# Reading the moving operand of the large matmuls in turns of four columns from its two halves

## The chip, the cores and the metric

The kernel runs on one core of one Trainium2 chip. The metric is device time in microseconds (us) for one launch. The time before is the median of two runs, 2388.72 us (2388.01 and 2389.42).

## The reference

The reference is one step of a two-layer transformer trunk in float32, applied to two groups of 128 tokens: a prompt, which has no cached context, and a sample, which has 128 cached positions. Layer 0 mixes tokens by latent attention and grouped-query attention side by side, layer 1 by differential attention; each layer ends with a gated feed-forward block with a width-3 convolution over positions. Cut to the parts that carry the work:

```python
for l in range(DEPTH):                                   # 2 layers
    mod = jax.nn.silu(cond) @ w_ada[l] + b_ada[l]        # 2048 x 12288, one row per group
    sh1, sc1, gt1, sh2, sc2, gt2 = jnp.split(mod[:, None, :], 6, axis=-1)
    h = rmsnorm(x, g_norm_mix[l]) * (1 + sc1) + sh1
    m, new = mixer_ab(h, ...) if l % 2 == 0 else mixer_c(h, ...)   # w_in, attention, w_out
    x = x + gt1 * m
    h = rmsnorm(x, g_norm_ffn[l]) * (1 + sc2) + sh2
    u = h @ w_ffn_up[l]                                  # 2048 x 11264
    u = conv3(u) + b
    x = x + gt2 * ((silu(gate) * val) @ w_ffn_down[l])   # 5632 x 2048
return rmsnorm(x, g_final), ab_ctx, c_ctx
```

Both groups use the same weights, so the kernel lays the two groups' 128 tokens beside each other: 256 columns, the first 128 for the prompt and the last 128 for the sample.

## The kernel before

**The product.** All large weight matrices are multiplied by `gemm` (lines 300 to 314) or, for the first three output blocks of a stage, by `first_three` (lines 279 to 298). An output block is 128 features by 256 tokens and is summed in one PSUM tile `acc` over blocks of 128 input features. To get near float32 accuracy out of the fp32r format, weights and activations are each split into a high and a low part. Each input block then takes three matmuls: high weights by high activations (L309, in `first_three` L295), high weights by low activations (L310, L296) and low weights by high activations (L313, L297). In each, the weights (128x128, `wh` or `wl`) are the stationary operand, loaded by a weight load of their own, and the activations (128x256) are the moving operand that streams past them. The moving operand is the tile `hx` (normalised input, also the attention output of layer 0), `g` (the gated hidden features), `oall` (attention output of layer 1) or `ql` (query latents), each with 256 high columns followed by 256 low ones for a block. One tile, `kv_in`, has 384 columns, since cached positions stand between the two groups.

**Where the operands lie.** Within a partition the high half of a moving operand is 256 contiguous float32 values, 1024 bytes, of which each group's 128 columns are 512 bytes. One weight block is 128 contiguous values, 512 bytes. The pools hold small tiles named `pad` (among them `SHIFT // 4` columns in L659, L910 and L1023, beside 48 columns in L112), and in the built program every moving operand of these matmuls begins at a byte address of 96 modulo 512 and every weight block at 160 modulo 512. `hx`, for one, lies at 42592, and the four buffers of `wh` at 118944, 123040, 127136 and 131232.

**What feeds it.** SyncE issues one DMA of 1 MB for each sixteen weight blocks (`raw`). ScalarE rounds 1024 columns of it to fp32r (`wh`, L216) and VectorE subtracts to get the low part (`wl`, L217). Four buffers each of `wh` and `wl` and three of `raw` lie between these engines and TensorE. Results leave PSUM through ScalarE or VectorE: a convolution with three taps in the feed-forward block (L1030, L1033, L1036), an addition into `x` behind the second product (L586).

**What stands between.** The modulation vectors `mod` need `w_ada`, 2048 x 12288 for each layer. Its work is strewn between the large products by `pump`, `row_step` and `feature_step`: some on TensorE (L434, plain float32 products with 32 weight columns), some on VectorE (L419, L463). Attention's own products (L635, L951, L970 and their neighbours) are plain float32.

**What sets the order.** The order on each engine comes from a planner that works from program order and a model of costs; some instructions are pinned to program order. The planner's order for the changed kernel is the same, instruction for instruction, on TensorE, VectorE, ScalarE, GpSimd and SyncE; besides the access patterns only a few waits on an engine that another wait already covers differ.

Of the kernel before, what the change touches and what calls it, by code (L numbers as in the profile page):

```python
# [20 lines left out]
T = 128  # L21
NT = 2 * T
ROW = 2 * NT
SHIFT = 448
NL = 2
GRID_W = 64
EPS = 1e-6
# [11 lines left out]
    ("rch", 128), ("rsh", 128), ("rcm", 128), ("rsm", 128),  # L39
    ("cond", 32), ("bada", NL * 6 * KD),  # L40
    ("gmix", NL * KD), ("gffn", NL * KD), ("gfin", 16),
    ("gmq", 6), ("gmkv", 4), ("gqn", 1), ("gkn", 1), ("lam", 4),
# [41 lines left out]
def step_kernel(ctx: ExitStack, tc: tile.TileContext, A: dict):  # L84
    nc = tc.nc
    pe, dve, act, pool, sp = nc.tensor, nc.vector, nc.scalar, nc.gpsimd, nc.sync
# [16 lines left out]
    def nm(s):  # L103
        uid[0] += 1
        return f"{s}_{uid[0]}"

    def T_(pl, shape, tag, dt=F32, bufs=None):
        kw = {} if bufs is None else {"bufs": bufs}
        return pl.tile(shape, dt, tag=tag, name=nm(tag), **kw)
# [8 lines left out]
    def C(name):  # L118
        a, w = _AT[name]
        return cst[:, a:a + w]  # L120
# [8 lines left out]

    mod = T_(keep, [P, NL, 6, KD, 2], "mod")  # L130
    scl = T_(keep, [P, NL, 2, KD, 2], "scl")

# [53 lines left out]
    def bank():  # L186
        return T_(pmisc, [P, 512], "misc")

    def att_bank():
        return T_(ppool["att"], [P, 512], "att", bufs=3)  # L190
# [30 lines left out]
    class Weights:  # L221
# [29 lines left out]
        def chunk(self):  # L251
# [24 lines left out]
            out, self.blocks = self.blocks[:self.nblk], self.blocks[self.nblk:]  # L276
            return out

    def first_three(W, xh, xl, order, mid=None, fixed=False):


        pin = tc.keep_in_program_order if fixed else lambda i: i
        raws = [W.load() for _ in range(3)]
        ps = [T_(pacc, [P, 512], "acc") for _ in range(3)]
        blocks = {(c, h): W.halves(raws[c], 8 * h) for c, h in ((0, 0), (1, 0), (2, 0), (0, 1))}
        count = [0] * 3
        for n, (c, k) in enumerate(order):
            if mid and n == len(order) // 2:
                mid()
            if (c, k // 8) not in blocks:  # L290
                blocks[c, k // 8] = W.halves(raws[c], 8)
            wh, wl = blocks[c, k // 8][k % 8]
            a, b = count[c] == 0, count[c] == KD - 1
            count[c] += 1
            pin(pe.matmul(ps[c][:, :NT], wh, xh(k), start=a, stop=False))  # L295
            pin(pe.matmul(ps[c][:, :NT], wh, xl(k), start=False, stop=False))  # L296
            pin(pe.matmul(ps[c][:, :NT], wl, xh(k), start=False, stop=b))  # L297
        return [p[:, :NT] for p in ps]

    def gemm(blocks, xh, xl, n=NT, first=0, between=None):  # L300


        fixed = lambda i: tc.keep_in_program_order(i) if between else i
        ps = T_(pacc, [P, 512], "acc")
        last = len(blocks) - 1
        for i in range(last + 1):
            k = (i + first) % (last + 1)
            wh, wl = blocks[k]
            fixed(pe.matmul(ps[:, :n], wh, xh(k), start=(i == 0), stop=False))  # L309
            fixed(pe.matmul(ps[:, :n], wh, xl(k), start=False, stop=False))  # L310
            if between and i == (last + 1) // 2:
                between()
            fixed(pe.matmul(ps[:, :n], wl, xh(k), start=False, stop=(i == last)))  # L313
        return ps[:, :n]


# [37 lines left out]
    def vector(name, l, j, q):  # L354

        at = (l * _AT[name][1] // NL) + j * KD + 4 * q
        return C(name)[:, at:at + 4, None].to_broadcast([P, 4, 2])
# [186 lines left out]
    def modulated(st, l, which, W, fixed):  # L544
# [29 lines left out]
        def turn():  # L574
            rest[1](tc.keep_in_program_order)

        ps = first_three(W, lambda k: hx[:, k, :NT], lambda k: hx[:, k, NT:2 * NT],
                         AS_MADE if fixed else IN_TURN, lambda: sum_rows(2, raws[2]), fixed)
        if fixed:
# [75 lines left out]
    def mixer_ab(hx, rb0, st):  # L655
        l = 0
        with tc.tile_pool(name="ab", bufs=1) as ab:
            with tc.tile_pool(name="abp", bufs=1) as pj:
                T_(ab, [P, SHIFT // 4], "pad")  # L659
                kv_in = T_(ab, [P, 4, 2, 3 * T], "kv_in", F32R)  # L660
# [104 lines left out]
                def part(W, k0, n, first, rate, between=None, **kw):  # L765

                    for c in range(23):
                        ps = gemm(W.chunk(), lambda k: hx[:, k0 + k, :NT], lambda k: hx[:, k0 + k, NT:2 * NT])
                        to = pr[:, c] if c < 15 else qb[:, c - 15]
                        if first:  # L770
                            act.copy(to, ps)
                        else:
                            dve.tensor_tensor(out=to, in0=to, in1=ps, op=ALU.add)
                        if between:
                            between(c)
                        pump(rate, **kw)
# [34 lines left out]
            with tc.tile_pool(name="abh", bufs=1) as hp:  # L811
# [35 lines left out]
                for h in range(8):  # L847
                    if h % 2 == 0:
                        for i in range(2):
                            ps = gemm(WQ.chunk(), qh, qlo)  # L850
                            qn[h + i] = T_(hp, [P, NT], "qn", bufs=4)
                            act.copy(qn[h + i], ps)
                            pump(RATE["heads"])
                        ps = gemm(WQ.chunk(), qh, qlo)
                        ev = T_(tmp, [P, NT], "nt", bufs=4)
                        act.copy(ev, ps)
                        qr = T_(hp, [P, NT], "qr", bufs=2)
                        act.copy(qr[:, 0:T], ev[:, 0:T])
                        rope(qr[:, None, T:], ev[:, None, T:], 1, 32, "rcm", "rsm")
                        pump(RATE["heads"])  # L860
# [34 lines left out]
    def mixer_c(cp, hx, W, ready, todo, st):  # L895
# [13 lines left out]
        product = lambda: ready.pop(0) if ready else gemm(W.chunk(), xh, xl, between=todo.pop(0) if todo else None)  # L909
        T_(cp, [P, SHIFT // 4 - 24], "pad")  # L910
        o_all = T_(cp, [P, KD, ROW], "oall", F32R)
# [90 lines left out]
        W = Weights(A["w_out_c"], KD, 1)  # L1002
        oh, ol = (lambda k: o_all[:, k, :NT]), (lambda k: o_all[:, k, NT:2 * NT])
        ready = first_three(W, oh, ol, LAST_LATE)
        for c in range(KD):
            fine[0] = c >= KD - QUIET[2]
# [8 lines left out]
    def ffn(hx, W, ready, todo, l, st):  # L1015
# [4 lines left out]
        with tc.tile_pool(name=f"ffn{l}", bufs=1) as fp, banks(f"pffn{l}") as pf:  # L1020
            feat["home"], feat["pool"] = fp, pf
            feat["due"] = 0.0
            T_(fp, [P, SHIFT // 4], "pad")  # L1023

# [53 lines left out]
    with banks("pab") as ppool["ada"]:  # L1078
# [4 lines left out]
        ps = [bank(), att_bank()]  # L1083
# [75 lines left out]
def _layout(i):  # L1159
# [29 lines left out]

    a["w_ada"] = i["w_ada"].reshape(NL, 4, 4, P, 6, 4, 512).transpose(0, 4, 5, 1, 3, 2, 6).copy()  # L1190
    for j in (1, 0):
# [60 lines left out]
```

## Time and profile before

| what | value |
|---|---|
| runs | 2388.01 and 2389.42 us, median 2388.72 |
| span of the profiled execution, first to last instruction | 2384.0 us |
| median of the runs less that span | 4.7 us |
| TensorE matmuls busy (union of overlapping matmuls) | 2333.9 us, 98% |
| TensorE weight loads busy | 2201.5 us, 92% |
| VectorE busy | 1775.5 us, 74% |
| ScalarE busy | 1164.9 us, 49% |
| DMA | 612.94 MB, mean 257 GB/s |
| mean granted TensorE clock | 0.994 |

The profile gives no time of the profiled execution other than its span; the 4.7 us around it are taken from the runs. Matmuls are pipelined: one is listed with some 0.28 us while the next begins 0.11 us after it. The busy share of TensorE therefore says whether the engine was ever without a matmul, and not how fast matmuls follow each other; that is read from the starts of neighbouring rows in the timeline.

### The profile page before, as it was taken

How to read it: one execution, taken by the hardware profiler on the slowest of the kernel's cores; microseconds unless marked ns; L12 is line 12 of the kernel's file. 1: busy time of each engine (PE TensorE's matmuls, PEld its weight loads, DVE VectorE, ACT ScalarE, POOL GpSimd, SP SyncE). 2: the span in 40 equal slices, each digit the busy share in tenths (PEclk: the TensorE clock that was granted, in tenths of full speed). 3: DMA queues.
4: the chain of work that ended last, by engine and by line, in shares of the span. 5: the costliest groups of instructions: out<-in, count | busy, mean ns of one | idle time of the engine just before them, and what ended most of it. 6: DMA issues, size and time to landing. Idle time of an engine off the chain costs nothing. (4 is left out here: it accounts for less than half of the span.)

```text
span 2384.0 us, 47535 instructions
## 1 busy us (share of the span) xinstructions
PE 2333.9 (98%) x19784; PEld 2201.5 (92%) x19784; DVE 1775.5 (74%) x2720; ACT 1164.9 (49%) x1817; POOL 167.6 (7%) x205
## 2 busy tenths in 40 slices
PE   8999999999999999999999999999999999999997
PEld 6778868789999999999989999998999999999997
DVE  2667545569999999999979777878899855666654
ACT  4345544365554345554455444445655534555542
POOL 0001101100000000001220000023000000000011
PEclk9999999999999999999999999999999999999999
DMA  8886678877777876777766787776767655555553
GB/s 347 352 336 250 226 282 310 317 269 260 261 253 282 296 278 252 265 263 270 297 238 235 277 295 293 257 300 265 257 250 261 212 194 193 193 194 193 194 194 123
DMA packets 92551, 612.94 MB, mean 257 GB/s; under 512 B 9969, under 2 KB 17841, under 8 KB 20529
## 3 DMA queue, kind: packets, MB, share of 16 engines
q1 hardware_dynamic: 92336, 609.91, 69.7%
q8 instruction: 155, 2.54, 0.4%
q14 instruction: 60, 0.48, 0.1%
HBM read 605.12 MB, written 4.75 MB: 256 GB/s over the span
## 5 line engine op out<-in xcount | busy, mean ns | idle before, releaser
L216 ACT CAST wh<-raw 128x1024 fp32r<-128x1024 f32 (+1 forms) x788 | 793.7, 1013 | 963.8 <-PE acc L310 803.0
L217 DVE TENSOR_TENSOR wl<-raw,wh 128x1024 fp32r<-128x1024 f32 (+1 forms) x788 | 921.2, 1182 | 368.9 <-ACT wh L216 363.1
L309 PE MATMUL acc<-hx,wh 128*128 128x256 f32 x4064 | 1132.3, 279 | 10.9 <-ACT wh L216 4.2
L313 PE MATMUL acc<-hx,wl 128*128 128x256 f32 x4064 | 1129.1, 278 | 0.8 <-DVE wl L217 0.8
L310 PE MATMUL acc<-hx,wh 128*128 128x256 f32 x4064 | 1128.3, 278 | 0.0
L309 PEld LDWEIGHTS acc<-hx,wh 128*128 128x128 f32 x4064 | 764.4, 188 | 40.9 <-issue 16.3
L313 PEld LDWEIGHTS acc<-hx,wl 128*128 128x128 f32 x4064 | 764.3, 188 | 11.8 <-issue 8.7
L310 PEld LDWEIGHTS acc<-hx,wh 128*128 128x128 f32 x4064 | 764.9, 188 | 9.4 <-issue 7.9
L310 PE MATMUL acc<-g,wh 128*128 128x256 f32 x1408 | 388.3, 276 | 0.0
L313 PE MATMUL acc<-g,wl 128*128 128x256 f32 x1408 | 388.0, 276 | 0.0
L309 PE MATMUL acc<-g,wh 128*128 128x256 f32 x1408 | 387.8, 276 | 0.0
L419 DVE CUSTOM_DVE_ANT_0 junk<-araw,condb 128x2048 f32<-128x2048 f32 x120 | 274.6, 2289 | 0.0
L310 PEld LDWEIGHTS acc<-g,wh 128*128 128x128 f32 x1408 | 264.3, 188 | 0.0
L313 PEld LDWEIGHTS acc<-g,wl 128*128 128x128 f32 x1408 | 264.1, 188 | 0.0
L309 PEld LDWEIGHTS acc<-g,wh 128*128 128x128 f32 x1408 | 264.0, 188 | 0.0
L172 POOL TENSOR_TENSOR sqacc<-sqacc,sq 128x256 f32<-128x256 f32 x62 | 82.0, 1322 | 1521.7 <-issue 1216.1
L463 DVE SCALAR_TENSOR_TENSOR aacc<-araw,condw,aacc 128x512 f32<-128x512 f32 x150 | 111.3, 767 | 0.2
L586 DVE SCALAR_TENSOR_TENSOR x<-acc,mod,x 128x128 f32<-128x128 f32 x192 | 58.1, 343 | 56.0 <-PE acc L313 55.0
L1030 ACT ACTIVATE cv<-acc,convw 128x256 f32<-128x256 f32 x176 | 98.3, 558 | 1.4 <-PE acc L297 1.4
L434 PE MATMUL ada<-araw,condw 128*32 128x512 f32 x704 | 94.6, 614 | 3.8 <-DMA araw<-w_ada 3.0
L1036 DVE SCALAR_TENSOR_TENSOR cv<-acc,convw,cv 128x254 f32<-128x254 f32 x176 | 84.2, 479 | 3.5
L1033 DVE SCALAR_TENSOR_TENSOR cv<-acc,convw,cv 128x254 f32<-128x254 f32 x176 | 83.5, 475 | 2.6 <-ACT cv L1030 2.5
(236 smaller groups left out, 1893.0 us busy)
## 6 DMA issues: line engine op xcount, KB each, us to landing
araw<-w_ada SPq DMA_DIRECT2D x186, 1024.0 KB, 5.8
raw<-w_up SPq DMA_DIRECT2D x176, 1024.0 KB, 4.8
raw<-w_down SPq DMA_DIRECT2D x88, 1024.0 KB, 4.8
raw<-w_in_c SPq DMA_DIRECT2D x48, 1024.0 KB, 5.3
raw<-w_in_ab SPq DMA_DIRECT2D x19, 1024.0 KB, 7.0
raw<-w_out_ab SPq DMA_DIRECT2D x16, 1024.0 KB, 6.8
raw<-w_out_c SPq DMA_DIRECT2D x16, 1024.0 KB, 4.8
raw<-w_ada SPq DMA_DIRECT2D x6, 1024.0 KB, 9.9
```

Source lines behind the costliest of these rows:

```text
L172: pool.tensor_tensor(out=st["acc"], in0=st["acc"], in1=sq, op=ALU.add)
L216: pin(act.copy(out_hi, src))
L217: pin(dve.tensor_tensor(out=out_lo, in0=src, in1=out_hi.bitcast(F32), op=ALU.subtract))
L309: fixed(pe.matmul(ps[:, :n], wh, xh(k), start=(i == 0), stop=False))
L310: fixed(pe.matmul(ps[:, :n], wh, xl(k), start=False, stop=False))
L313: fixed(pe.matmul(ps[:, :n], wl, xh(k), start=False, stop=(i == last)))
L419: tc.keep_in_program_order(dve.tensor_tensor_reduce(out=T_(feat["pool"], [P, D], "junk"), in1=feat["row"][:, c], in0=feat["raw"].rearrange ...
L434: i = pe.matmul(ada["ps"][32 * g:32 * g + 32, :], condw[:, 4 * t + g, :], raw[:, g], start=(t == 0), stop=(t == 3), skip_group_check=True)
L463: i = dve.scalar_tensor_tensor(out=acc[:, c], in0=raw[:, g], scalar=condw[:, k, c:c + 1], in1=acc[:, c], op0=ALU.mult, op1=ALU.add)
L1030: pin(act.activation(y, ps, AF.Identity, scale=cw[:, 1, m:m + 1], bias=cw[:, 3, m:m + 1]))
L1033: pin(dve.scalar_tensor_tensor(out=y3[:, :, 1:], in0=p3[:, :, :T - 1], scalar=cw[:, 0, m:m + 1], in1=y3[:, :, 1:], op0=ALU.mult, op1=ALU.add))
L1036: pin(dve.scalar_tensor_tensor(out=y3[:, :, :T - 1], in0=p3[:, :, 1:], scalar=cw[:, 2, m:m + 1], in1=y3[:, :, :T - 1], op0=ALU.mult, op1=A ...
```

## The change

The 256 columns of a moving operand are no longer read from first to last. They are read in turns of four: columns 0 to 3 of the first half, columns 0 to 3 of the second half, columns 4 to 7 of the first half, and so on, 64 turns in all. The output pattern is permuted in the same way, so each result lands in the same place of PSUM as before. For `kv_in` the turns go over three blocks of 128. The weight operand, the number of instructions and all other instructions stay as they are. Half the lines added are the same edit in `first_three`.

```diff
+RUN = 4
...
+    def paired(ap):
+
+        return ap.rearrange("p (j i e) -> p i j e", i=T // RUN, e=RUN)
+
...
+            out = paired(ps[c][:, :NT])
-            pin(pe.matmul(ps[c][:, :NT], wh, xh(k), start=a, stop=False))
+            pin(pe.matmul(out, wh, paired(xh(k)), start=a, stop=False))
...
         ps = T_(pacc, [P, 512], "acc")
+        out = paired(ps[:, :n])
         last = len(blocks) - 1
         for i in range(last + 1):
             k = (i + first) % (last + 1)
             wh, wl = blocks[k]
-            fixed(pe.matmul(ps[:, :n], wh, xh(k), start=(i == 0), stop=False))
-            fixed(pe.matmul(ps[:, :n], wh, xl(k), start=False, stop=False))
+            fixed(pe.matmul(out, wh, paired(xh(k)), start=(i == 0), stop=False))
+            fixed(pe.matmul(out, wh, paired(xl(k)), start=False, stop=False))
             if between and i == (last + 1) // 2:
                 between()
-            fixed(pe.matmul(ps[:, :n], wl, xh(k), start=False, stop=(i == last)))
+            fixed(pe.matmul(out, wl, paired(xh(k)), start=False, stop=(i == last)))
         return ps[:, :n]
```

More of the change, by code (lines that the diff above doesn't have):

```diff
@@ L294, in first_three @@
             count[c] += 1
-            pin(pe.matmul(ps[c][:, :NT], wh, xh(k), start=a, stop=False))
-            pin(pe.matmul(ps[c][:, :NT], wh, xl(k), start=False, stop=False))
-            pin(pe.matmul(ps[c][:, :NT], wl, xh(k), start=False, stop=b))
+            out = paired(ps[c][:, :NT])
+            pin(pe.matmul(out, wh, paired(xh(k)), start=a, stop=False))
+            pin(pe.matmul(out, wh, paired(xl(k)), start=False, stop=False))
+            pin(pe.matmul(out, wl, paired(xh(k)), start=False, stop=b))
         return [p[:, :NT] for p in ps]
```

## The prediction

> **What bounds the kernel now.** First the page's busy times, then two long stretches of the windows view, taken from the feed-forward blocks, then TensorE's waits.
>
> ```profile
> span 2384.0 us, 47535 instructions
> PE 2333.9 (98%) x19784; PEld 2201.5 (92%) x19784; DVE 1775.5 (74%) x2720; ACT 1164.9 (49%) x1817; POOL 167.6 (7%) x205
> PEclk9999999999999999999999999999999999999999
> ```
>
> ```profile
> core 0: us, PE busy (x) PEld busy (x) DVE busy (x) ACT busy (x) POOL busy (x), PEclk, DMA share, GB/s
> 700.00:1100.00 400.00, 400.00 (x3532) 400.00 (x3531) 368.05 (x462) 195.26 (x250) 0.00 (x0) 1.00 0.74 272
> 1700.00:2300.00 600.00, 600.00 (x5297) 600.00 (x5296) 428.28 (x558) 298.65 (x388) 6.73 (x5) 1.00 0.60 212
> ```
>
> ```profile
> PE misc L1088 <- ACT sq L1086: 6.7, 1, 6.7
> PE acc L309 <- ACT wh L216: 4.2, 2, 2.7
> PE att L197 <- ACT sq L168: 3.9, 3, 2.4
> ```
>
> TensorE is without a matmul for only 2384.0 - 2333.9 = 50 us, and its longest waits in all are a few us each, so nothing upstream sets the time. In both stretches matmuls follow each other at the same pace, 400/3532 = 0.113 us and 600/5297 = 0.113 us, although VectorE is busy 92% in one and 71% in the other, and DMA 0.74 and 0.60. The clock is at its full grant. The pace of a large product is thus a property of the product, and the end is set by that pace times their number. The timeline gives the pace more exactly (the 54 starts from the first row to the last all belong to such products):
>
> ```profile
> 999.80 0.28 PE L310 MATMUL acc<-hx,wh 128*128 128x256 f32 x1
> ...
> 1000.03 0.28 PE L309 MATMUL acc<-hx,wh 128*128 128x256 f32 x1
> ...
> 1005.92 0.28 PE L310 MATMUL acc<-hx,wh 128*128 128x256 f32 x1
> ```
>
> (1005.92 - 999.80)/54 = 0.1133 us for 256 columns, 0.443 ns a column. [...]
>
> How many there are, from the groups by line and shape. L310 and L313 have the count of L309, and L295 and L297 that of L296:
>
> ```profile
> L309 PE MATMUL acc<-hx,wh 128*128 128x256 f32 x4064 | 1132.3, 279 | 10.9 <-ACT wh L216 4.2 <-ACT hx L537 2.5 <-ACT cv L1030 2.5
> L309 PE MATMUL acc<-g,wh 128*128 128x256 f32 x1408 | 387.8, 276 | 0.0
> L309 PE MATMUL acc<-oall,wh 128*128 128x256 f32 x208 | 57.9, 279 | 0.0
> L296 PE MATMUL acc<-hx,wh 128*128 128x256 f32 x144 | 41.4, 293 | 3.1 <-POOL hx L522 2.7
> L309 PE MATMUL acc<-ql,wh 128*128 128x256 f32 x72 | 20.8, 288 | 0.0
> L296 PE MATMUL acc<-oall,wh 128*128 128x256 f32 x48 | 14.0, 293 | 0.0
> L309 PE MATMUL acc<-kv_in,wh 128*128 128x384 f32 x64 | 22.7, 355 | 0.0
> ```
>
> Three times (4064 + 1408 + 208 + 144 + 72 + 48) = 17,832 products of 256 columns, 2021 us at 0.1133, or 85% of the span; and 192 of 384 columns. One nanosecond more or less a product is 17.8 us.
>
> **Is there anything to gain in 0.1133?** Two comparisons say that there is. The 384-column products, ten steps apart, and attention's plain float32 products among the large ones:
>
> ```profile
> 229.21 0.34 PE L310 MATMUL acc<-kv_in,wh 128*128 128x384 f32 x1
> ...
> 230.94 0.34 PE L313 MATMUL acc<-kv_in,wl 128*128 128x384 f32 x1
> ```
>
> ```profile
> 1251.61 1.47 PE L951 MATMUL att<-dk,dq 128*128 128x128 f32 x8
> ```
>
> ```profile
> L951 PE MATMUL att<-dk,dq x64: 270/327/382, 1251.6 to 1536.7; 128*128 128x128 f32 x32, 128*128 128x256 f32 x32
> ```
>
> 384 columns take 0.173 us: half as many columns again cost 0.060 us more, 0.467 ns each, above the mean of 0.443 of the first 256. So a constant cost per product is not all that stands over the columns; something grows with them. The eight float32 passes (four of 128 columns, four of 256) start over 1.47 - 0.38 = 1.09 us before the last one; that is ten times 128 columns, 0.109 us each. A float32 pass streams at half the fp32r pace, so 128 of its columns take as many steps as 256 here, and it has a 128-column weight load beside it too. It needs 4.3 ns less.
>
> What differs? A weight load's duration grows from 32 to 128 columns as follows:
>
> ```profile
> L434 PEld LDWEIGHTS ada<-araw,condw 128*32 128x32 f32 x704 | 14.5, 108 | 19.3 <-issue 6.1 <-DMA araw<-w_ada 3.2 <-DVE scl L400 1.2
> L309 PEld LDWEIGHTS acc<-g,wh 128*128 128x128 f32 x1408 | 264.0, 188 | 0.0
> ```
>
> (188 - 108)/96 = 0.83 ns a column, 107 ns for a block. During one product, therefore, weights are read through 512 bytes once, while the moving operand passes through 1024 bytes. Both begin at fixed places modulo 512 (96 and 160). I read the excess as the two readers of SBUF meeting: modulo 512 the moving reader goes at twice the weight reader's speed and overtakes it once a product, and a 384-column one overtakes more often. In the float32 pass both go through 512 bytes in the same time and neither overtakes. This reading is inferred; no row shows a bank.
>
> **The change part by part.** *Reading.* The halves lie 512 bytes apart, so a turn of four from each keeps both on one place modulo 512, which moves through 512 bytes once a product: the speed of the weight reader. They start 64 bytes apart and stay so; if they do touch, a stall draws them apart, and they don't catch up again. On this reading the product goes to the float32 pass's pace: 113.3 - 109 = 4.3 ns, times 17,832 = 77 us. The bounds: nothing removed (0 us), and on the other side the prices of the rivals below. I take the 109 because it is the only row in which a 128-column weight load stands beside 256 steps of streaming at equal speeds. The weight load allows it: 107 ns.
>
> [...]
>
> *The 384-column products.* 192 times at most some 10 ns, 2 us; I count nothing, as three blocks of 128 don't run level with the weights.
>
> *Writing.* PSUM receives the same 256 values in the same places, in runs of 16 bytes. I cost it at nothing; no row shows a matmul that writes in broken runs, so the bounds are nothing and the half pace of the fourth rival.
>
> *Order.* Every engine's instructions stand in the same order as before, SyncE's DMAs and GpSimd's included; nothing moves past a queue, and no wait is added. Conv, residual and attention read PSUM as before.
>
> *What takes back.* VectorE in the first stretch is busy 368 of 400 us; with the stretch 4% shorter it is at 96%. ScalarE's wait there shows that the weights are ahead of TensorE:
>
> ```profile
> ACT wh L216 <- PE acc L310: 173.8, 120, 1.9
> ```
>
> It waited 174 us of 400 for a weight buffer to be released, so the split isn't late on average; but bursts of VectorE's 2.3 us feature sums (L419) will now make TensorE wait here and there. DMA goes from 0.74 to 0.77. Waits in attention and at the ends of stages keep their length. I take a fifth off: 77 - 15 = 62 us. Span 2384.0 - 62 = 2322; with the 4.7 us by which the median of the runs is above the span, **2327 us**, 2.6% faster. Own range: 2310 (all of it) to 2345 (just over half).
>
> **The rivals.**
>
> *No change* (2389 us, say 2380 to 2395). The excess belongs to the product and not to a meeting of two readers: 256 columns and a turnover of fixed length, or a limit of the read port at 4 bytes a step, which the float32 pass at half the pace never reaches. For: the pace is the same to the nanosecond whichever tile is read. Against a fixed turnover alone: the 384-column rows. The change not doing what it says would also end here; the built program has the permuted patterns on both operands, so I give that nothing of its own.
>
> *Lockstep collision* (slower). Level speeds are good only if the readers are apart by more than what they share. The start addresses differ by 64 bytes, but the address that the reader is at, at a given moment, depends on skews which no row shows. Now they close at 1024/113 - 512/109 = 4.4 bytes a ns. If they disturb each other within 64 bytes, the overtaking lasts 2 x 64/4.4 = 29 ns and costs 4.3, 15%. Disturbed throughout, a product takes 109 x 1.15 = 125 ns, 12 more than now: 17,832 x 12 = 214 us, 2603. With a narrower shared place the same cost falls on less time and the price per ns is higher; up to 2750. It decides against the change from 2.7 ns over the present pace (48 us). Against it: a stall draws the readers apart.
>
> *One step a turn* (slower). If the address generation or the line fetch loses one step of 0.443 ns at each of the 64 turns, that is 28 ns a product, 506 us: 2895. Nothing in the trace reads a matmul operand in broken runs, so nothing excludes it.
>
> *Half pace of the writes* (slower). The only half pace in this trace is the float32 pass's: 256 columns at twice 0.109, 105 ns more a product, 1.87 ms: about 4260.
> [...]
>
> **How the numbers follow.** Meeting removed 0.44 (0.42 of it beyond 2%), no change 0.18, lockstep collision 0.18 (0.02 of it within 2%), one step a turn 0.10, half pace 0.10. Within 2% (about 48 us, what a measurement of this kernel can tell from no change) is 0.02 + 0.18 + 0.02 = 0.22; slower 0.16 + 0.10 + 0.10 = 0.36; faster 0.42. The range must reach past "no change" to the collision, 2305 to 2750, and leaves out the last two rivals, 0.20.
>
> **What would show it.** In the timeline of a feed-forward stretch, neighbouring products start 109 ns apart if I am right, 113 if nothing changes, 125 and more for a collision, 142 for a step a turn, 218 for half pace. The 384-column products should move by less, as a share, than the 256-column ones. If the pace falls and the time doesn't, TensorE's waits on `wl` (L217) must have grown. The forecast is wrong if the excess isn't a meeting of readers, or if broken runs have a price of their own in reading or writing; both show in the pace alone.

## The result and the profile after

The changed kernel takes 2611.85 us (2610.76 and 2612.94) against 2388.72: 1.093 times as long, with a 95% interval of 1.090 to 1.096. Forecast was 2327 us; the time lies inside the stated range, on the other side of no change.

The page of the changed kernel, its busy times and granted clock:

```profile
span 2610.8 us, 47527 instructions
PE 2562.7 (98%) x19784; PEld 2430.7 (93%) x19784; DVE 1786.2 (68%) x2720; ACT 1181.4 (45%) x1817; POOL 161.8 (6%) x205
PEclk9999999999999999999999999999999999999999
```

The same two kinds of stretch in the windows view (both lie wholly in feed-forward blocks, columns as before):

```profile
700.00:1100.00 400.00, 400.00 (x3160) 400.00 (x3159) 334.27 (x412) 175.95 (x220) 0.00 (x0) 1.00 0.66 242
1900.00:2500.00 600.00, 600.00 (x4739) 600.00 (x4739) 378.99 (x492) 269.64 (x345) 3.93 (x3) 1.00 0.53 186
```

The instruction counts of TensorE, VectorE and ScalarE on the page are those of before, and TensorE is idle for 48 us where it was 50. Only the pace is another: 400/3160 = 600/4739 = 0.1266 us a product. The timeline shows that the pace has also become uneven; steps from 0.12 to 0.14 us follow each other, where the kernel before kept to 0.113 in the same kind of stretch:

```profile
999.85 0.29 PE L320 MATMUL acc<-hx,wl 128*128 128x256 f32 x1
999.97 0.29 PE L316 MATMUL acc<-hx,wh 128*128 128x256 f32 x1
...
1005.67 0.30 PE L316 MATMUL acc<-hx,wh 128*128 128x256 f32 x1
1005.81 0.29 PE L317 MATMUL acc<-hx,wh 128*128 128x256 f32 x1
```

And the products of 384 columns went from 0.173 to 0.196 us: five of them lie between the starts 251.93 and 252.91 of the timeline.

The sum: 17,832 products times 126.6 - 113.3 = 13.3 ns are 237 us, 192 times 23 ns are 4; together 241 us, where the span grew by 226.8. So the growth is in the pace of the products, and the sum is 14 us too high. A part of these 14 us shows in the kernel before: not all of its products kept 113.3 ns. Here are two of its runs between attention's products, on the same tile:

```profile
1266.28 0.28 PE L309 MATMUL acc<-hx,wh 128*128 128x256 f32 x1
...
1271.04 0.28 PE L309 MATMUL acc<-hx,wh 128*128 128x256 f32 x1
...
1272.53 0.28 PE L309 MATMUL acc<-hx,wh 128*128 128x256 f32 x1
...
1280.31 0.28 PE L309 MATMUL acc<-hx,wh 128*128 128x256 f32 x1
```

The first two rows are 42 products apart, the last two 66: (1271.04 - 1266.28)/42 = 113.3 ns and (1280.31 - 1272.53)/66 = 117.9 ns. By the starts in the trace, over 1,200 products of the kernel before stand in runs at about 118 ns, which makes 5 to 6 us. The rest of the 14 us was not followed further.

### The profile page after: what moved, and what is told of

Same layout as the page of the kernel before. It is cut to its first block, busy times and chain, and to the rows that moved or that the text cites. A ratio compares the mean times of both kernels' runs of the same rounds, so it can differ in the third digit from the quotient of the medians.

```text
span 2610.8 us, 47527 instructions
## 1 busy us (share of the span) xinstructions
PE 2562.7 (98%) x19784; PEld 2430.7 (93%) x19784; DVE 1786.2 (68%) x2720; ACT 1181.4 (45%) x1817; POOL 161.8 (6%) x205
## 4 chain that ended last, share of the span: by engine, by line
PE 96%; issue 1%; DVE 1%; DMA 1%; ACT 1%; POOL 0%; POOLq 0%; DVEq 0%; ACTq 0%
PE acc L316 28%; PE acc L320 28%; PE acc L317 28%; PE ada L441 3%; PE acc L302 1%; PE acc L301 1%; PE acc L303 1%; PE att L642 1%; DMA raw<-w_in_ab 0%; PE att L958 0%; PE ada L389 0%; PE att L632 0%; PE misc L441 0%; PE misc L1095 0%; ACT wh L217 0%
## 5 line engine op out<-in xcount | busy, mean ns | idle before, releaser
L217 ACT CAST wh<-raw 128x1024 fp32r<-128x1024 f32 (+1 forms) x788 | 812.2, 1036 | 1176.9 <-PE acc L317 982.2
L316 PE MATMUL acc<-hx,wh 128*128 128x256 f32 x4064 | 1191.7, 294 | 10.8 <-ACT wh L217 4.2
L320 PE MATMUL acc<-hx,wl 128*128 128x256 f32 x4064 | 1188.6, 293 | 0.3 <-DVE wl L218 0.2
L317 PE MATMUL acc<-hx,wh 128*128 128x256 f32 x4064 | 1187.7, 292 | 0.0
L316 PEld LDWEIGHTS acc<-hx,wh 128*128 128x128 f32 x4064 | 772.6, 190 | 40.6 <-issue 17.2
L320 PEld LDWEIGHTS acc<-hx,wl 128*128 128x128 f32 x4064 | 773.0, 190 | 11.3 <-issue 8.7
L317 PEld LDWEIGHTS acc<-hx,wh 128*128 128x128 f32 x4064 | 773.2, 190 | 9.4 <-issue 7.9
L317 PE MATMUL acc<-g,wh 128*128 128x256 f32 x1408 | 409.6, 291 | 0.0
L320 PE MATMUL acc<-g,wl 128*128 128x256 f32 x1408 | 409.3, 291 | 0.0
L316 PE MATMUL acc<-g,wh 128*128 128x256 f32 x1408 | 409.1, 291 | 0.0
L317 PEld LDWEIGHTS acc<-g,wh 128*128 128x128 f32 x1408 | 267.1, 190 | 0.0
L316 PEld LDWEIGHTS acc<-g,wh 128*128 128x128 f32 x1408 | 266.9, 190 | 0.0
```

Of the source, the lines that this page charges most:

```text
L217: pin(act.copy(out_hi, src))
L316: fixed(pe.matmul(out, wh, paired(xh(k)), start=(i == 0), stop=False))
L317: fixed(pe.matmul(out, wh, paired(xl(k)), start=False, stop=False))
L320: fixed(pe.matmul(out, wl, paired(xh(k)), start=False, stop=(i == last)))
```

## The experiments

Two theories of the forecast's list fit a pace of 126 ns at first sight: the lockstep collision, which had been priced at 125 ns and 2603 us, and a price for every turn, a part of a step in place of a whole one. Against both stood that it might be the writing. Each time of a whole kernel below is that of one run; the kernel before took 2387.26 us on the same chip beside the first three of them, and 2388.07 on another chip beside the later three.

### Reading alone and writing alone

Only the output, or only the moving operand, stays in turns. The tokens of each result then stand in another order than the computation wants, with the same work to do.

```diff
 read_only:
-        out = paired(ps[:, :n])
+        out = ps[:, :n]
 write_only:
-            fixed(pe.matmul(out, wh, paired(xh(k)), start=(i == 0), stop=False))
+            fixed(pe.matmul(out, wh, xh(k), start=(i == 0), stop=False))
 ...
```

> The moving operand is read in turns of four as in the changed kernel, but the 256 results are written to PSUM in unbroken order, so the tokens of each result stand in the order of the turns. If the price is in the reading (lockstep collision with the weight load, or a part of a step for each turn), a product takes about 126 ns and the time stays near 2612 us. If it is in the writing, the product goes back to about 113 ns (or 109, if the reading has won something) and the time to 2389 us (or 2320).

> The moving operand is read in unbroken order, the 256 results are written to PSUM in turns of four, so the tokens of each result stand in the order of the turns. If the price is in the reading: 113 ns and 2389 us. If it is in the writing: 126 ns and 2612 us.

Measured: 2617.65 us with the reading in turns, 2388.97 with the writing in turns. The windows view of reading alone, then of writing alone:

```profile
700.00:1100.00 400.00, 400.00 (x3160) 400.00 (x3159) 333.90 (x413) 175.15 (x219) 0.00 (x0) 1.00 0.67 244
```

```profile
700.00:1100.00 400.00, 400.00 (x3532) 400.00 (x3531) 368.09 (x460) 195.21 (x250) 0.00 (x0) 1.00 0.74 272
```

3160 and 3532 products in 400 us: the counts of the changed kernel and of the kernel before. The whole price is in the reading; writing 256 results to PSUM in runs of sixteen bytes costs nothing (2388.97 us against 2387.26). So the fourth rival is out.

### Longer turns

```diff
-RUN = 4
+RUN = 16
```

> Turns of sixteen columns in place of four, on both sides, 16 turns a product in place of 64. A price for each turn (0.21 ns each by the 13.3 ns of the changed kernel) gives 113.3 + 3.3 = 116.7 ns and about 2445 us. Lockstep collision gives still about 126 ns and 2612 us, since turns of sixteen also pass through the 512 bytes at the weight load's speed, in steps of 64 bytes. A price for the step to a new place that depends on which place it is could lie anywhere between.

Measured: 2490.93 us; 400/3336 = 119.9 ns a product:

```profile
700.00:1100.00 400.00, 400.00 (x3336) 400.00 (x3335) 352.27 (x437) 183.03 (x233) 0.00 (x0) 1.00 0.70 257
```

Neither number. A quarter of the turns leaves half of the price, so the price isn't so much for each turn; and it isn't what a collision that lasts the whole product would give either.

### Series of products by themselves: offsets, weights and turns

A kernel of series of 60 matmuls in place of the computation, each series with an output tile of its own name (the code is shortened here):

```diff
+    def series(name, off, n=NT, read=same, write=same, weight=None, ...):
+        for i in range(count):
+            m = mv[:, 512 * (i % 8) + off:512 * (i % 8) + off + n]
+            w = weight(i) if weight else wt[:, P * (i % 16):P * (i % 16) + P]
+            pin(pe.matmul(write(ps[:, :n]), w, read(m), ...))
+    for k, letter in enumerate("abcdefgh"):
+        series("plain" + letter, off=16 * k)
+    for k, letter in enumerate("abcdefgh"):
+        series("four" + letter, off=16 * k, read=four, write=four)
+    ...
+    still = lambda i: wt[:, 0:1].to_broadcast([P, P])
+    series("fourstill", off=112, weight=still, read=four, write=four)
```

> Only series of 60 matmuls of the large products' kind, back to back, on fp32r tiles of the input, in place of the whole computation; the outputs are set to zero. Weights at 160 modulo 512, the moving operand at eight offsets of 64 bytes from them, read and written plainly (plain a to h) and in turns of four (four a to h); h is the kernel's placement, in which 113 and 127 ns are expected. Lockstep collision: the pace in turns of four changes strongly with the offset, down to about 109 ns somewhere, and goes to 109 to 113 where all weight columns are read from one address (fourstill). A price for each turn: the same at all eight offsets and with weights from one address, and halved with each doubling of the turn (two, eight, sixteen, thirtytwo, sixtyfour: 140, 120, 117, 115, 114 ns). A price of writing: writefour as fourh, readfour as plainh. If the excess of 113 over 109 is a meeting with the weight reader, plainstill shows 109 and the plain pace changes with the offset; if it belongs to the reading itself, plainstill shows 113.

The timeline of this kernel merges each series into one row (start, time from the first start to the last end, output, number of matmuls). The pace is the distance to the next row's start over 60:

```profile
27.47 7.37 PE L117 MATMUL plaina<-mv,wt 128*128 128x256 f32 x60
34.67 7.23 PE L117 MATMUL plainb<-mv,wt 128*128 128x256 f32 x60
41.74 7.28 PE L117 MATMUL plainc<-mv,wt 128*128 128x256 f32 x60
48.86 6.96 PE L117 MATMUL plaind<-mv,wt 128*128 128x256 f32 x60
55.66 7.34 PE L117 MATMUL plaine<-mv,wt 128*128 128x256 f32 x60
...
77.03 6.96 PE L117 MATMUL plainh<-mv,wt 128*128 128x256 f32 x60
83.83 7.78 PE L117 MATMUL foura<-mv,wt 128*128 128x256 f32 x60
...
129.73 7.94 PE L117 MATMUL fourg<-mv,wt 128*128 128x256 f32 x60
137.51 7.76 PE L117 MATMUL fourh<-mv,wt 128*128 128x256 f32 x60
145.10 7.77 PE L117 MATMUL readfour<-mv,wt 128*128 128x256 f32 x60
152.71 6.98 PE L117 MATMUL writefour<-mv,wt 128*128 128x256 f32 x60
159.52 10.36 PE L117 MATMUL runtwo<-mv,wt 128*128 128x256 f32 x60
169.71 7.57 PE L117 MATMUL runeight<-mv,wt 128*128 128x256 f32 x60
177.12 7.36 PE L117 MATMUL runsixteen<-mv,wt 128*128 128x256 f32 x60
184.32 7.29 PE L117 MATMUL runthirtytwo<-mv,wt 128*128 128x256 f32 x60
...
214.17 6.99 PE L117 MATMUL plainstill<-mv,wt 128*128 128x256 f32 x60
220.99 7.63 PE L117 MATMUL fourstill<-mv,wt 128*128 128x256 f32 x60
228.46 6.98 PE L117 MATMUL plainstart<-mv,wt 128*128 128x256 f32 x60
```

Series h stands as the kernel's tiles do and has its two paces: (83.83 - 77.03)/60 = 113 ns plainly, (145.10 - 137.51)/60 = 127 in turns. What the reader is to see:

- **Weights do matter to the plain order, and the kernel before stood at the best place.** Offsets a, b, c and d give 120, 118, 119 and 113 ns, and the four go round once more: the pattern repeats every 256 bytes. The offset between moving operand and weights costs up to 7 ns a product, but nothing in the long stretches of the kernel before. With all weight columns read from one address the excess is gone, as series of the next kernel show (113.7 ns over the offsets a to d).
- **They matter little to the turns of the changed kernel.** The eight offsets give 126.5 to 129.7 ns (h is the cheapest, g the dearest), and with all weight columns read from one address it is still (228.46 - 220.99)/60 = 124.5. Of the 13 ns, two (126.5 - 124.5) go when the weights are read from one address. The lockstep collision is out.
- **The 113 doesn't go with the weights' addresses either.** With weights from one address the plain order stays at (220.99 - 214.17)/60 = 113.7.
- **Not so much a turn.** Turns of 2, 4, 8 and 16 columns cost 170, 127, 123 and 120 ns; twice as long a turn doesn't halve the excess.

### What the price goes by

Both remaining theories speak of the reader alone: a price of the break, or one of the place. A line below means the sixteen bytes, four columns, that one turn reads. The code is shortened again:

```diff
+    nested = lambda ap: ap.rearrange("p (i e) -> p i e", e=4)
+    series("nested", off=112, read=nested)
+    series("oneplace", read=lambda ap: ap[:, 0:4][:, None, :].to_broadcast([P, 64, 4]), ...)
+    for parts, letter in ((4, "quarters"), (8, "eighths"), (16, "sixteenths"), ...):
+        series("by" + letter, read=lambda ap: turns(ap, 4, parts), ...)
+    for apart in (4, 8, 16, 32, 48, 64):    # halves 512 + 4 * apart bytes from each other
+        series("apart" + letter, wide=2 * apart, read=read, ...)
+    for k, letter in enumerate("abcd"):
+        series("still" + letter, off=16 * k, weight=still)
+    series("full", full=True, ...)          # plain float32
```

> Series of 60 matmuls as in bench1, all written to PSUM in unbroken order; the outputs of the computation are set to zero. Reading in turns of four costs 13 ns a product there, whatever the offset from the weights. Two theories are left. A price of the break: the reader loses part of a step whenever a run ends, wherever it goes on. Then 126 to 127 ns also where all 64 turns read the same sixteen bytes (oneplace), at every distance between neighbouring turns (bythirtyseconds 32 bytes, bysixteenths 64, byeighths 128, byquarters 256, apart one to sixteen 528 to 768 bytes), with few weights (fourfew), and nothing in plain float32 at half the pace (fullfour as full, 215 ns) if the loss is hidden there. A price of the place: successive reads that fall on the same bank of SBUF, which by bench1 repeats every 256 bytes, have to wait. Then oneplace is dearest or, if a line once read is kept, 113; 512 bytes and byquarters are dear, and distances of 64, 128 or 192 bytes beyond 512 (apart four, eight, twelve) go back to about 113. The 113 itself: if it is a meeting with the weight load, plainfew (32 weight columns) is at 109 and still a to d (weights from one address) change with the offset; if it belongs to the reading of fp32r, both stay at 113, and 512 columns (wide) take 227 ns.

Its timeline, read in the same way:

```profile
27.98 7.23 PE L119 MATMUL nested<-mv,wt 128*128 128x256 f32 x60
35.05 6.86 PE L119 MATMUL oneplace<-mv,wt 128*128 128x256 f32 x60
41.74 8.38 PE L119 MATMUL byquarters<-mv,wt 128*128 128x256 f32 x60
49.96 7.59 PE L119 MATMUL byeighths<-mv,wt 128*128 128x256 f32 x60
57.39 7.02 PE L119 MATMUL bysixteenths<-mv,wt 128*128 128x256 f32 x60
64.25 7.26 PE L119 MATMUL bythirtyseconds<-mv,wt 128*128 128x256 f32 x60
71.35 7.61 PE L119 MATMUL apartone<-mv,wt 128*128 128x256 f32 x60
...
86.19 7.48 PE L119 MATMUL apartfour<-mv,wt 128*128 128x256 f32 x60
93.51 7.57 PE L119 MATMUL aparteight<-mv,wt 128*128 128x256 f32 x60
...
233.93 6.98 PE L119 MATMUL stilla<-mv,wt 128*128 128x256 f32 x60
...
261.22 7.66 PE L119 MATMUL fourstilla<-mv,wt 128*128 128x256 f32 x60
...
291.13 7.17 PE L119 MATMUL plainfew<-mv,wt 128*32 128x256 f32 x60
298.14 7.89 PE L119 MATMUL fourfew<-mv,wt 128*32 128x256 f32 x60
...
333.77 17.43 PE L119 MATMUL full<-mv,wt 128*128 128x256 f32 x80
351.03 17.43 PE L119 MATMUL fullfour<-mv,wt 128*128 128x256 f32 x80
```

`oneplace` has as many turns as the changed kernel, all on the same sixteen bytes, and takes (41.74 - 35.05)/60 = 111.5 ns: **the break itself is free.** The rest goes by where the next line lies: 114 ns when each turn goes 64 bytes on, 118 at 32 bytes, 124 at 128, 137 at 256. At 128 bytes most of it goes when all weights are read from one address: that order then takes (137.65 - 130.65)/60 = 116.7 ns (`byeighthsstill`), while steps of 256 bytes still take (130.65 - 122.62)/60 = 133.8. Halves of 528, 576 and 640 bytes' distance in place of 512 cost 124, 122 and 123 (the rows behind the first and the third of these begin at 78.79 and 100.91): an excess of 9 to 11 ns in place of 13, and not the return to about 113 that the theory of the place expected. Plain float32, which takes half the pace, (351.03 - 333.77)/80 = 216 ns, takes the same in turns (both rows last 17.43 us): at half the pace the turns cost nothing. With a weight load of 32 columns the plain order is not at 109 but at 117; 512 columns (from 305.87 to 319.86) take 233 ns, 0.455 a column, and 232 with weights from one address.

Four series with weights from one address, `stilla` to `stilld`, read plainly at the offsets a to d; together they take (261.22 - 233.93)/240 = 113.7 ns a product. So the 118 to 120 ns of offsets a to c are gone once the weights are read from one address. But the offset alone doesn't set the pace: `nested` reads the same columns in the same plain order at the kernel's own offset, its pattern only written as 64 fours on end, and takes (35.05 - 27.98)/60 = 117.8 ns where series h took 113. The plain order thus has a second pace of about 118 at the very place of the kernel, as in the runs between attention's products. What decides between the two wasn't followed.

### The distance, in the whole computation

The same 64 turns of the same lines, with another step from turn to turn, on both sides of the product:

```diff
-        return ap.rearrange("p (j i e) -> p i j e", i=T // RUN, e=RUN)
+        return ap.rearrange("p (j i e) -> p i j e", i=4, e=RUN)     # step64
+        return ap.rearrange("p (j i e) -> p i j e", i=16, e=RUN)    # step256
```

> The whole computation in turns of four as in the changed kernel, on both sides, but the turns follow each other at 64 bytes (all first lines of the 64-byte blocks, then all second ones, and so on): the same 64 turns of the same lines, another order. If the price is that of a turn as such: 126.7 ns and 2612 us as before. If it goes by the distance to the next line, as in the series (114.5 ns at 64 bytes): 1.2 ns a product over the kernel before, 2388 + 21 = about 2410 us.

> As step64, but the turns follow each other at 256 bytes, four to a round. Price of a turn as such: 126.7 ns and 2612 us. By the distance, as in the series (137.4 ns): 24 ns a product, 2388 + 429 = about 2817 us.

Measured: 2393.51 us with steps of 64 bytes, 2770.15 with steps of 256. First the window of the one, then of the other:

```profile
700.00:1100.00 400.00, 400.00 (x3498) 400.00 (x3497) 364.08 (x456) 191.87 (x246) 0.00 (x0) 1.00 0.73 269
```

```profile
700.00:1100.00 400.00, 400.00 (x2962) 400.00 (x2961) 314.76 (x388) 163.02 (x202) 0.00 (x0) 1.00 0.64 230
```

114.4 and 135.0 ns a product. With as many turns as the changed kernel, one order costs 1 ns a product and the other 22, against 13: the price goes by the step between successive lines and not by the number of turns, in the kernel as in the series. Both times came out below the sums (2410 and 2817), as that of the changed kernel did.

### The weights at another place

```diff
-    T_(wpool, [P, 48], "pad", bufs=1)
+    T_(wpool, [P, 64], "pad", bufs=1)
```

> The kernel before, reading plainly, with one edit: sixteen columns more in the pad ahead of the weights, so that the weights lie 64 bytes higher, at 224 modulo 512; hx stays at 96, the other moving tiles move along. Only hx's 12,624 products see another distance to the weights, 128 bytes. If moving reads and weight reads disturb each other by their places, as in the series (118.6 ns at that distance), hx's products go from 113.3 to about 118.6 and the time to 2388 + 67 = about 2455 us, while g's stay at 113.3. If the places don't matter in the whole kernel, 2388 us.

Measured: 2443.61 us. A window in which only `hx` streams, and one of `g`'s products alone (the first column in brackets counts them):

```profile
900.00:1000.00 100.00, 100.00 (x845) 100.00 (x844) 89.86 (x117) 50.45 (x71) 0.00 (x0) 1.00 0.69 251
```

```profile
700.00:900.00 200.00, 119.85 (x1056) 119.78 (x1056) 2.90 (x7) 2.77 (x7) 1.00 0.75 278
```

118.3 ns for `hx`, 119.85/1056 = 113.5 for `g`, which kept its distance to the weights. In the whole kernel too the pace goes by that distance, and sixteen columns of padding decide about 55 us (2443.61 - 2388.07).

### Is there anything left under 113?

```diff
+    for apart, letter in ((4, "sixteen"), ..., (64, "twofiftysix"), (128, "fivetwelve")):
+        series("two" + letter, read=two, weight=still, ...)      # two lines, to and fro
+    series("fourtwofiftysix", read=lines, weight=still, ...)     # four lines
+    for k, letter in enumerate("abcdefghijklmnop"):
+        series("plain" + letter, off=8 * k)
+        series("step" + letter, off=8 * k, read=step)      # steps of 64 bytes
```

> Series of 60 matmuls as in bench1; the outputs of the computation are set to zero. First, turns of four that go to and fro between the same two lines of sixteen bytes, 16 to 512 bytes apart (two sixteen to two fivetwelve), and between four lines 256 bytes apart (fourtwofiftysix), all with the weights read from one address. If two places that are equal modulo 256 bytes exclude each other as such, two lines 256 or 512 bytes apart cost as much as in the changed kernel (124 ns) and four of them 134, while 64 and 128 bytes apart cost 112 to 113. If the price is that of going on to new lines, all are at 112, as sixteen bytes read 64 times were. Then the plain order and the order of 64-byte steps (step) at sixteen offsets of 32 bytes from the weights. If an offset is left at which the reading costs less than the 113.3 ns of the kernel before, there is something to win; if 113.3 is the reader's own pace for fp32r, none is.

```profile
55.38 6.86 PE L119 MATMUL twotwofiftysix<-mv,wt 128*128 128x256 f32 x60
62.08 6.86 PE L119 MATMUL twofivetwelve<-mv,wt 128*128 128x256 f32 x60
68.78 8.77 PE L119 MATMUL fourtwofiftysix<-mv,wt 128*128 128x256 f32 x60
...
245.97 6.96 PE L119 MATMUL stepi<-mv,wt 128*128 128x256 f32 x60
252.77 7.05 PE L119 MATMUL stepj<-mv,wt 128*128 128x256 f32 x60
```

Two lines to and fro cost 111.7 ns at 256 and at 512 bytes, like a single line; four lines 256 bytes apart cost (77.38 - 68.78)/60 = 143, the next row beginning at 77.38. So lines equal modulo 256 bytes don't exclude each other as such; a pair of lines that comes again is free, and four that come again are dearer than any other fp32r order of whole lines here. Why halves at 576 bytes' distance still cost 122 ns stays open. Of sixteen offsets in two orders none is below the (252.77 - 245.97)/60 = 113.3 of `stepi`; the kernel's own place, `plaino`, has (183.50 - 176.67)/60 = 113.8. No order measured that reads all 256 columns beats the 113 ns of the kernel before; what is left in it are its runs at 118, 5 to 6 us.

## Why the prediction was wrong

**What bounds the kernel: right.** The end is set by the pace of the large products times their number. The pace rose by 13.3 ns, which makes 241 us by the prediction's own count, and 226.8 were measured; no wait took its place.

**"Is there anything to gain in 0.1133?" is the step that failed.** I read the 4.3 ns above attention's float32 pass as the moving reader overtaking the weight reader; no run shows an overtaking. The weights' place does change the pace (118 to 120 ns at the offsets a to c), but at the 64 bytes of the built program the 113 is already what the plain order takes with all weights from one address (113.7). The comparison itself was at fault. A float32 pass streams at half the pace (216 ns for 256 columns), and `full` and `fullfour` show that at half the pace even the turns are free (17.43 us both); it says nothing of what an fp32r product could do. The prediction had named this possibility under "no change" (a limit of the reader which the float32 pass never reaches), and the series fit that part of the rival as far as they go: turns that cost 13 ns at the full pace cost nothing at half of it. No run shows a limit of the reader itself. The 384-column rows, which I took for more overtaking, fit a pace that belongs to reading as well: 512 columns cost 0.455 ns each, and hardly less with weights from one address (0.453). No fp32r series here that reads all 256 columns came under 113.3.

The trace before held a sign that was overlooked. The prediction says that the pace is the same to the nanosecond whichever tile is read, but `hx` has runs at 118 beside those at 113. A second, slower pace at the same place spoke for 113 as the better of two paces, not for 109 below it. What makes these runs slower, no run shows.

**The value of the reading: wrong in sign.** From the removed meeting I took -4.3 ns; the turns cost +13.3. The lower bound of the term was "the prices of the rivals", and they held it. The lockstep rival had 125 ns and 2603 us, very near the 126.6 and 2612 measured, but that is luck, for the runs refute its reason: with the weights read from one address 11 of the 13 ns remain (124.5 against 113.7). The rival of one step a turn had the right side, the reading, and the wrong law: the price goes by the distance of successive lines, so 64 turns cost 1 ns or 22.

**Writing at nothing: right**, 3532 products in 400 us with the writing in turns. **The order and the upstream engines: right**; they slackened with TensorE (VectorE 68% of the span after 74%), so the fifth taken off for them never came into play.

**The chances.** 0.44 rested on one float32 row at another pace. The kernel's placement, equal for all tiles, was in the prediction; that the long stretches at this place already kept the pace which the plain order has with weights from one address (113.3 ns there, 113.7 in the series) was the reading that I didn't give a chance of its own.

## What to carry to other kernels

Before a gain is drawn from a faster row of another kind, ask whether that row puts the same load on the part in question: here the float32 pass took 216 ns in order and in turns, the fp32r product 113 and 127. For fp32r products of 256 columns that follow each other without a gap, read the moving operand in order (113.3 ns here), or in steps of 64 bytes where another order is needed (114.4); permute the output in PSUM instead if a permutation can go on either side (400/3532 = 113.3). Where moving and stationary operands are at a fixed distance modulo 256 bytes, a few columns of padding are worth measuring (here sixteen columns were worth 55 us).

## What the runs showed of the hardware that I had not expected

- Sixteen bytes read 64 times take 111.5 ns, a plain kilobyte 113.3, and the same kilobyte with steps of 256 bytes 137 in the series.
- Turns of two columns, half a line each, cost 170 ns in the series: here the price jumps.
- Plain reading depends on the weights' place with a period of 256 bytes: 120, 118, 119 and 113 ns. At the place of the 113 it can also run at 118 for a whole series or for over a hundred products.
- Products of 32 weight columns were slower than those of 128 (117 against 113 ns at the same offset), although each loads a quarter of the weights.
